# Moving the norm chains, the token sums and two groups of loads by hand in a one-core decoder layer

## The chip, the core and the metric

One NeuronCore of a Trainium2 chip runs one layer of a hybrid decoder as one program. The metric is the device time of a launch in microseconds. The engines that matter here are TensorE (PE, matrix products), VectorE (DVE), ScalarE (ACT), GpSimd (POOL) and the queue of SyncE (SP), which issues most loads and stores. Each engine works through its own list in order; semaphores tie the lists together.

## The reference, cut to what matters

All arithmetic is fp32. The attention part, which the change does not touch, yields a mixed row `m` per token. What follows is this:

```python
xp = xp + rms_norm(m @ w_o, norm_mix_post)            # 1024 x 1024
h = rms_norm(xp, norm_ffn_pre)
z = h @ w_in                                          # 1024 x (2 * 2816)
g, u = split(z, 2)
c = sum(conv_w[j] * g_padded[:, j:j + T] for j in range(3)) + conv_b
y = (gelu(c) * u) @ w_out                             # 2816 x 1024
y_out = xp + rms_norm(y, norm_ffn_post)
```

`rms_norm(x, g)` is `x * rsqrt(mean(x*x) + eps) * g`, with the mean over a token's 1024 features.

## The kernel before

The 1032 tokens (1024 of the prompt, 8 samples) lie along the free axis, in three segments `s` = 0, 1, 2 of 344; the features lie on the 128 partitions in eight blocks `d`. A factor of a product is split into two reduced-precision parts (`wh`, `wl` for weights, `hh`, `hl` for rows), and each product takes three matmuls. One block of 128 outputs by one segment is therefore 24 matmuls (8 blocks of the contraction, 3 each), which the text calls a unit.

**Output projection.** For each segment, eight units `ps_o` are computed (d = 0..7). ACT copies each result to `mix`, squares it, and POOL adds the square to `acc`.

**The norm chain** of a segment, the generator `norms_stage(s, acc, mix)`, then does: `rstd_1` (PE sums `acc` over the partitions into `n`; DVE scales it to `ms`; POOL takes the power -1/2, `rr`; DVE splits that into `rs` and builds the diagonal matrices `dg`), `rstd_2` (two matmuls spread the diagonals over all partitions, `bc`), then for each d `mix *= bc`, `x1 = x + mix` (even d on POOL, odd d on DVE) and the squares into `acc2`; then `rstd_1` and `rstd_2` again, and for each d `ht = x1 * g * bc`, its rounded part `hh[s]` (ACT) and the rest `hl[s]` (DVE). The text calls the four PE pieces of the chain of segment s n1(s), bc1(s), n2(s) and bc2(s). The `yield`s let the caller weave the chain into the products: two steps after each unit, and what is left at the end of a segment.

**The MLP's opening.** `ffn_in(j, s, ...)` computes a gate unit `gp` and an up unit `up` for column block j and segment s. It runs for j = 0, 1 on segments 0 and 1 with chain 2 woven in, then for j = 0, 1 on segment 2. Between them stand the **token sums**: from the rows of segments 0 and 1 (`hh`, `hl`), POOL forms for each of k = 0..3 the sums `tt` which `put` splits into `tw[0..2]` (ACT rounds, DVE subtracts) and back into `hh[1]`. The block loop j = 2..21 (`block`) needs `tw`, and weight sums `S1..S4` that POOL forms and `put` splits into `ww`.

**The last stage** multiplies by `w_out` (`ps_y`, loads by `load_t` and `load_n`: weights `wyraw`, rows `ar`). The chains of its two parts, `finish(part, acc, fv, x1)`, scale `fv` on DVE, add `x1y` on POOL and store `yT` on the SP queue, behind which the next loads stand.

Where nothing fixes it, a scheduler orders each engine's list. Before the change PE's list is in program order only from the block loop on.

Of the kernel before, what the change touches and what calls it, by code (L numbers as in the profile page):

```python
# [51 lines left out]
def step_kernel(ctx: ExitStack, tc: tile.TileContext, gam, g128, xT, w_in, w_o, w_f, w_y, norms, ngb, cst, subln,  # L52
# [777 lines left out]
    def norms_stage(s, acc, mix):  # L830

        yield
        dg = rstd_1(pw, acc)
# [30 lines left out]
        for d in range(ND):  # L864
            t = pw.tile([P, SEG], F32, tag="sq", bufs=3, name="ht")
            nc.vector.scalar_tensor_tensor(t, x1[:, d, :], gn[:, 2, d:d + 1], bc, ALU.mult, ALU.mult)
            nc.scalar.activation(a[:, d, 2:SEG + 2], t, AF.Copy)
            nc.vector.tensor_tensor(b[:, d, 2:SEG + 2], t, a[:, d, 2:SEG + 2].bitcast(F32), ALU.subtract)
            if d % 2 and d < ND - 1:
                yield  # L870
# [4 lines left out]
    chain = None
    rot = 0
    w_all = [*w2, split_w(load_w(w_o[2]), wo, "o", bufs=6)]
    for s in range(3):
# [3 lines left out]
        for d in range(ND):  # L882
# [13 lines left out]
            add_sq(pw, acc, ps, d == 0, nc.gpsimd)  # L896
            if chain is not None and (d, s) not in first:
                next(chain, None)
                next(chain, None)
        if chain is not None:  # L900
            for _ in chain:
                pass
        chain = norms_stage(s, acc, mix)
# [64 lines left out]
    for j in range(2):  # L968
        for s in range(2):
            for _ in ffn_in(j, s, *wj[j]):  # L970
                next(chain, None)
                next(chain, None)
    for _ in chain:
        pass
# [9 lines left out]
    def part(t, s, k):
        return t[s][:, k, 2:SEG + 2].bitcast(F32)

    def put(hi, lo, t):
        nc.scalar.activation(hi, t, AF.Copy)  # L988
        nc.vector.tensor_tensor(lo, t, hi.bitcast(F32), ALU.subtract)  # L989

    for k in range(4):
        b12, b22, t1, t2, t3 = (tt.tile([P, SEG], F32, tag=f"tt{i}", name=f"tt{i}") for i in range(5))
        G = nc.gpsimd.tensor_tensor
        G(b12, part(hh, 1, k), part(hl, 1, k), ALU.add)
        G(b22, part(hh, 1, 4 + k), part(hl, 1, 4 + k), ALU.add)
        G(t3, b22, b12, ALU.subtract)
        put(tw[1][:, 0, k], tw[1][:, 1, k], t3)
        G(t1, b12, part(hh, 0, k), ALU.subtract)
        G(t1, t1, part(hl, 0, k), ALU.subtract)
        G(t2, b22, t1, ALU.subtract)  # L1000
        put(tw[0][:, 0, k], tw[0][:, 1, k], t2)
        G(b12, part(hh, 0, 4 + k), t2, ALU.subtract)
        G(b12, b12, part(hl, 0, 4 + k), ALU.add)
        put(tw[2][:, 0, k], tw[2][:, 1, k], b12)
        put(hh[1][:, k, 2:SEG + 2], hl[1][:, k, 2:SEG + 2], t1)
# [397 lines left out]
```

## Time and profile before

| what | value |
|---|---|
| time, median of 3 runs | 1395.82 us (1395.66 to 1395.98) |
| the profiled execution's own time | 1393.19 us |
| its span | 1391.1 us |
| mean granted TensorE clock | 0.985 |
| busy: PE / DVE / ACT / POOL | 1317.4 / 980.6 / 574.4 / 494.7 us |

The profile records one execution. Its span runs from the first to the last instruction; the execution's own time has 2.1 us more around it. That execution was 2.6 us below the median of the runs, so a sum that is made on the span is carried to the median by differences. Times in the rows are microseconds from the start of the span.

### The profile page before, as it was taken

Reading aid. Unit: us, or ns where it says so; the run is one execution under the profiler, and the core shown is the slowest. Engines: PE = TensorE matmul, PEld = TensorE weight load, DVE = VectorE, ACT = ScalarE, POOL = GpSimd, SP = SyncE. Lnnn points to the kernel's source line nnn. Section 1 sums busy time; section 2 is a strip of 40 time slices with the busy share of each in tenths; the row PEclk is TensorE's granted clock in tenths of the full one; section 3 lists DMA queues with packets and bytes.
Section 4 is the critical chain, followed back from the end, with each engine's and each line's share of the span. In section 5 each row is a group of like instructions: output and inputs, shape, how many; then the busy total and the mean of one; then the engine's idle time right before and its main releaser. Section 6 shows DMA issues by size and latency. Waiting matters only on the chain.

```text
span 1391.1 us, 22792 instructions
## 1 busy us (share of the span) xinstructions
PE 1317.4 (95%) x8235; PEld 1270.0 (91%) x8235; DVE 980.6 (70%) x1832; ACT 574.4 (41%) x1148; POOL 494.7 (36%) x402
## 2 busy tenths in 40 slices
PE   6999989999999999998879999999999999989998
PEld 5999888888999999998879999999999999989976
DVE  7665759879688865478777777777777655565575
ACT  6254425335222145354344443443443345536544
POOL 5300356745545621444652332332432200140140
PEclk9999999999999999999989999999999999999999
DMA  5334275764564534233022222121122277667674
GB/s 220 118 102 134 85 238 195 218 202 126 163 192 142 176 120 160 71 113 109 29 92 79 81 97 74 69 91 68 70 91 69 84 259 261 211 210 251 188 235 156
DMA packets 96915, 196.51 MB, mean 141 GB/s; under 512 B 17306, under 2 KB 47130, under 8 KB 96418
## 3 DMA queue, kind: packets, MB, share of 16 engines
q1 hardware_dynamic: 90082, 183.45, 40.6%
q10 hardware_dynamic: 6720, 11.62, 2.3%
q8 instruction: 64, 1.05, 0.3%
q14 instruction: 49, 0.40, 0.1%
HBM read 155.11 MB, written 30.48 MB: 133 GB/s over the span
## 4 chain that ended last, share of the span: by engine, by line
PE 66%; DVE 16%; POOL 7%; DMA 5%; issue 4%; ACT 2%; SPq 0%; DVEq 0%; POOLq 0%; ACTq 0%
PE ps_y L1213 4%; PE ps_in L114 4%; PE ps_y L1212 4%; PE ps_y L1214 4%; PE ps_in L116 4%; PE ps_in L115 4%; DVE acc_v L587 3%; PE pb L1021 3%; PE pb L1020 3%; PE pb L1022 3%; PE up L1022 2%; PE pc L1021 2%; PE pc L1022 2%; PE up L1021 2%; PE pc L1020 2%
## 5 line engine op out<-in xcount | busy, mean ns | idle before, releaser
L114 PE MATMUL ps_in<-xh,wh 128*128 128x344 f32 x672 | 224.8, 335 | 6.8 <-ACT xh L193 5.9
L115 PE MATMUL ps_in<-xl,wh 128*128 128x344 f32 x672 | 221.2, 329 | 1.9 <-DVE xl L194 1.9
L116 PE MATMUL ps_in<-xh,wl 128*128 128x344 f32 x672 | 220.0, 327 | 1.1 <-DVE wl L109 1.1
L114 PEld LDWEIGHTS ps_in<-xh,wh 128*128 128x128 f32 x672 | 130.2, 194 | 9.9 <-ACT xh L193 5.9
L1153 DVE TENSOR_TENSOR wyl<-wyraw,wyh 128x1024 fp32r<-128x1024 f32 x66 | 83.7, 1271 | 74.1 <-ACT wyh L1152 71.8
L115 PEld LDWEIGHTS ps_in<-xl,wh 128*128 128x128 f32 x672 | 130.1, 194 | 4.4 <-DVE xl L194 3.6
L161 POOL TENSOR_TENSOR acc<-acc,sq 128x344 f32<-128x344 f32 (+1 forms) x56 | 59.0, 1054 | 208.8 <-ACT sq L160 203.9
L116 PEld LDWEIGHTS ps_in<-xh,wl 128*128 128x128 f32 x672 | 130.0, 193 | 1.6 <-DVE wl L109 1.4
L1212 PE MATMUL ps_y<-ah,wyh 128*128 128x388 f32 x352 | 120.2, 341 | 4.4 <-ACT ah L1163 4.4
L1039 POOL TENSOR_TENSOR S<-wraw 128x512 f32<-128x512 f32 x20 | 33.0, 1652 | 252.3 <-DMA wraw<-in_w_f 237.8
L1213 PE MATMUL ps_y<-al,wyh 128*128 128x388 f32 x352 | 120.1, 341 | 1.2 <-DVE al L1164 1.2
L1214 PE MATMUL ps_y<-ah,wyl 128*128 128x388 f32 x352 | 119.6, 340 | 0.0
L494 POOL TENSOR_TENSOR pg<-pg,qb 128x512 f32<-128x512 f32 x64 | 91.2, 1447 | 37.5 <-DMA pg<-in_kpool 26.9
L1152 ACT ACTIVATE wyh<-wyraw 128x1024 fp32r<-128x1024 f32 x66 | 69.7, 1058 | 73.8 <-PE ps_y L1213 43.5
L989 DVE TENSOR_TENSOR ww<-S,ww 128x512 fp32r<-128x512 f32 x80 | 88.6, 1125 | 9.1 <-ACT ww L988 9.1
L988 ACT ACTIVATE ww<-S 128x512 fp32r<-128x512 f32 x80 | 50.6, 634 | 94.2 <-POOL S L1040 33.9
L989 DVE TENSOR_TENSOR ww<-wraw,ww 128x512 fp32r<-128x512 f32 x80 | 75.2, 941 | 19.2 <-ACT ww L988 17.6
L1020 PE MATMUL pb<-tw,ww 128*128 128x344 f32 x240 | 77.3, 322 | 10.9 <-ACT tw L988 10.2
L988 ACT ACTIVATE ww<-wraw 128x512 fp32r<-128x512 f32 x80 | 50.1, 627 | 86.8 <-PE up L1022 63.4
L1164 DVE TENSOR_TENSOR al<-ar,ah 128x388 fp32r<-128x388 f32 (+2 forms) x110 | 60.5, 564 | 25.8 <-ACT ah L1163 24.9
L1021 PE MATMUL pb<-tw,ww 128*128 128x344 f32 x240 | 77.3, 322 | 0.8 <-DVE tw L989 0.8
L1022 PE MATMUL pb<-tw,ww 128*128 128x344 f32 x240 | 76.9, 321 | 0.0
(324 smaller groups left out, 3841.6 us busy)
## 6 DMA issues: line engine op xcount, KB each, us to landing
wyraw<-in_w_y SPq DMA_DIRECT2D x66, 512.0 KB, 3.8
wraw<-in_w_f SPq DMA_DIRECT2D x44, 512.0 KB, 3.2
pg<-in_kpool SPq DMA_DIRECT2D x64, 256.0 KB, 3.0
pg<-in_vpool SPq DMA_DIRECT2D x64, 256.0 KB, 2.7
wraw<-in_w_in SPq DMA_DIRECT2D x27, 512.0 KB, 4.1
ar<-ad SPq DMA_DIRECT2D x44, 194.0 KB, 3.8
ad<-cc SPq DMA_DIRECT2D x20, 344.0 KB, 2.3
ar<-ad SPq DMA_DIRECT2D x44, 150.0 KB, 3.3
```

The lines of the kernel that those rows point to most:

```text
L114: nc.tensor.matmul(ps, lhsT=wh[:, k, :], rhs=ah[:, k, n0:n1], start=(first and i == 0), stop=False)
L115: nc.tensor.matmul(ps, lhsT=wh[:, k, :], rhs=al[:, k, n0:n1], start=False, stop=False)
L116: nc.tensor.matmul(ps, lhsT=wl[:, k, :], rhs=ah[:, k, n0:n1], start=False, stop=(last and i == len(order) - 1))
L494: nc.gpsimd.tensor_tensor(kp, kp, qb.rearrange("p (a b) -> p a b", b=P), ALU.mult)
L988: nc.scalar.activation(hi, t, AF.Copy)
L989: nc.vector.tensor_tensor(lo, t, hi.bitcast(F32), ALU.subtract)
L1020: nc.tensor.matmul(ps, lhsT=w[:, 0, k], rhs=bh, start=(first and k == 0), stop=False, skip_group_check=True)
L1021: nc.tensor.matmul(ps, lhsT=w[:, 0, k], rhs=bl, start=False, stop=False, skip_group_check=True)
L1022: nc.tensor.matmul(ps, lhsT=w[:, 1, k], rhs=bh, start=False, stop=(last and k == 3), skip_group_check=True)
L1212: nc.tensor.matmul(pss[d], lhsT=wh[:, i, w], rhs=ah, start=(f == 0), stop=False)
L1213: nc.tensor.matmul(pss[d], lhsT=wh[:, i, w], rhs=al, start=False, stop=False)
L1214: nc.tensor.matmul(pss[d], lhsT=wl[:, i, w], rhs=ah, start=False, stop=(f == NF - 1))
```

## The change

It has five parts. (1) `rstd_1` builds all diagonals with one broadcast multiplication instead of two instructions per 128 columns. (2) `norms_stage` keeps `x` in four tiles of two rows with four buffers, each loaded and stored by itself, in place of one tile with one buffer; its squares have two buffers and `ht` two of its own; for segment 1 the rows before rounding stay as `h1`; for segment 2 the odd `hl` are subtracted on POOL. (3) The steps of a chain are set by a table, `STEPS`, one entry per unit behind the chain's start; chains may overlap; PE's list is in program order from the output projection on, with a list of accumulator banks written out. (4) The opening runs over segments outside and column blocks inside; the token sums are formed from `h1` with six POOL instructions per k instead of nine, k = 0, 1, 2 behind the units 3, 4 and 6 of the opening and k = 3 behind the chain; POOL's list there is in program order. (5) `finish` issues the store of row d - 2 behind the addition of row d.

```diff
-        dg = pl.tile([P, 2, n], F32R, tag="dg", bufs=1, name="dg")
-        for b, (c, w) in enumerate(blks):
-            for i in range(2):
-                nc.vector.tensor_scalar(dg[:, i, c:c + w], ident[:, 0:w], rs[:, i, b:b + 1].bitcast(F32), None,
-                                        ALU.mult)
-        return dg
+        dg = pl.tile([P, 2 * nb, P], F32R, tag="dg", bufs=1, name="dg")
+        nc.vector.tensor_tensor(dg, ident.unsqueeze(1).broadcast_to([P, 2 * nb, P]),
+                                rs.bitcast(F32).rearrange("p a b -> p (a b)").unsqueeze(2)
+                                .broadcast_to([P, 2 * nb, P]), ALU.mult)
+        return dg.rearrange("p (a b) c -> p a (b c)", a=2)[:, :, 0:n]
...
-        x1 = pw.tile([P, ND, SEG], F32, tag="x1", name="x1")
-        nc.sync.dma_start(x1, xT[s])
+        xp = [pw.tile([P, 2, SEG], F32, tag="x1", bufs=4, name="x1") for _ in range(4)]
+        x1 = [xp[d // 2][:, d % 2] for d in range(ND)]
+        for i in range(4):
+            nc.sync.dma_start(xp[i], xT[s, :, 2 * i:2 * i + 2])
...
+            (nc.gpsimd if s == 2 and d % 2 else nc.vector).tensor_tensor(
+                b[:, d, 2:SEG + 2], t, a[:, d, 2:SEG + 2].bitcast(F32), ALU.subtract)
...
+    STEPS = [{0: 1, 2: 2, 3: 2, 6: 1, 8: 2, 9: 2}] * 2 + [{0: 1, 2: 2, 3: 2, 5: 1, 7: 4}]
+    chains = []
+    def unit_done():
+        for ch in list(chains):
+            for _ in range(STEPS[ch[2]].get(ch[1], 0)):
+                next(ch[0], None)
+            ch[1] += 1
...
+    def token_sums(k):
+        t1, t2, t3, t4 = (tt.tile([P, SEG], F32, tag=f"tt{i}", bufs=(4 if i == 0 else 2), name=f"tt{i}")
+                          for i in range(4))
+        G = nc.gpsimd.tensor_tensor
+        G(t1, h1[k], hh[0][:, k, 2:SEG + 2].bitcast(F32), ALU.subtract)
+        G(t1, t1, hl[0][:, k, 2:SEG + 2].bitcast(F32), ALU.subtract)
+        t1s.append(t1)
+        G(t2, h1[4 + k], t1, ALU.subtract)
+        put(tw[0][:, 0, k], tw[0][:, 1, k], t2)
+        G(t3, h1[4 + k], h1[k], ALU.subtract)
+        put(tw[1][:, 0, k], tw[1][:, 1, k], t3)
+        G(t4, hh[0][:, 4 + k, 2:SEG + 2].bitcast(F32), t2, ALU.subtract)
+        G(t4, t4, hl[0][:, 4 + k, 2:SEG + 2].bitcast(F32), ALU.add)
+        put(tw[2][:, 0, k], tw[2][:, 1, k], t4)
+    for s in range(2):
+        for j in range(2):
+            for _ in ffn_in(j, s, *wj[j]):
+                unit_done()
+                if u in (3, 4, 6):
+                    token_sums({3: 0, 4: 1, 6: 2}[u])
+                u += 1
+    for ch in chains:
+        for _ in ch[0]:
+            pass
+    token_sums(3)
...
             nc.gpsimd.tensor_tensor(x1[:, d, :], x1[:, d, :], fv[:, d, :], ALU.add)
+            if d > 1:
+                nc.sync.dma_start(yT[part, :, d - 2, :], x1[:, d - 2, :])
+            yield
+        for d in (ND - 2, ND - 1):
             nc.sync.dma_start(yT[part, :, d, :], x1[:, d, :])
-            yield
```

Three places show how the lists move. The first is POOL's list in the opening, around the end of chain 2's additions. Before, the power `rr` of n2(2) came right behind the four even rows of `x1`, and the second group of token sums behind it:

```order
L842 TENSOR_TENSOR x1_8095<-x1_8095,mix_7825 128x344
L842 TENSOR_TENSOR x1_8095<-x1_8095,mix_7904 128x344
L131 TENSOR_TENSOR rr_8258<-ms_8256,ct_71 128x3
L994 TENSOR_TENSOR tt0_8394<-hh_7912,hl_7913 128x344
L996 TENSOR_TENSOR tt4_8398<-tt1_8395,tt0_8394 128x344
```

Of the change, the four even rows of `x1` are followed by the token sums of k = 0 and 1, twelve instructions. The piece below begins at the ninth of them; `rr` of n2(2) stands behind the twelfth, and the sums of k = 2 stand ahead of the odd `hl` of segment 2.

```order
L994 TENSOR_TENSOR tt1_8233<-h1_8068,tt0_8232 128x344
L996 TENSOR_TENSOR tt2_8234<-h1_8068,h1_8006 128x344
L998 TENSOR_TENSOR tt3_8235<-hh_7668,tt1_8233 128x344
L999 TENSOR_TENSOR tt3_8235<-tt3_8235,hl_7669 128x344
L131 TENSOR_TENSOR rr_8287<-ms_8285,ct_71 128x3
L991 TENSOR_TENSOR tt0_8319<-h1_8010,hh_7668 128x344
L992 TENSOR_TENSOR tt0_8319<-tt0_8319,hl_7669 128x344
L994 TENSOR_TENSOR tt1_8320<-h1_8072,tt0_8319 128x344
L996 TENSOR_TENSOR tt2_8321<-h1_8072,h1_8010 128x344
L998 TENSOR_TENSOR tt3_8322<-hh_7668,tt1_8320 128x344
L999 TENSOR_TENSOR tt3_8322<-tt3_8322,hl_7669 128x344
L871 TENSOR_TENSOR hl_8371<-ht_8378,hh_8370 128x344
```

What moved: `rr`, for which n2(2)'s chain waits, is now behind twelve token sums, and the rest of that chain behind six more.

The second is DVE's list there. Before, the last square of chain 2 was added (`acc`) ahead of the token sums' `tw`:

```order
L842 TENSOR_TENSOR x1_8095<-x1_8095,mix_7957 128x344
L161 TENSOR_TENSOR acc_8097<-acc_8097,sq_8185 128x344
L931 SCALAR_TENSOR_TENSOR c_8244<-gp_8194,cwt_7978,c_8244 128x344
L161 TENSOR_TENSOR acc_8097<-acc_8097,sq_8190 128x344
L932 SCALAR_TENSOR_TENSOR c_8244<-gp_8194,cwt_7978,c_8244 128x344
L989 TENSOR_TENSOR tw0_8367<-tt3_8376,tw0_8367 128x344
```

Of the change, two `tw` of k = 0 stand ahead of the last `acc`:

```order
L841 TENSOR_TENSOR x1_8111<-x1_8111,mix_7919 128x344
L983 TENSOR_TENSOR tw0_7962<-tt1_8192,tw0_7962 128x344
L983 TENSOR_TENSOR tw1_7963<-tt2_8193,tw1_7963 128x344
L160 TENSOR_TENSOR acc_8116<-acc_8116,sq_8187 128x344
L942 SCALAR_TENSOR_TENSOR c_8273<-gp_8207,cwt_7924,c_8273 128x344
```

Further on, the three `tw` of k = 2 and the returned rows of segment 1 stand between the diagonals of n2(2) and the first row `ht` of segment 2:

```order
L136 TENSOR_TENSOR dg_8292<-ct_71,rs_8289 128x768
L983 TENSOR_TENSOR tw0_7962<-tt1_8320,tw0_7962 128x344
L983 TENSOR_TENSOR tw1_7963<-tt2_8321,tw1_7963 128x344
L983 TENSOR_TENSOR tw2_7964<-tt3_8322,tw2_7964 128x344
L941 SCALAR_TENSOR_TENSOR c_8360<-gp_8294,cwt_7924,c_8360 128x344
L983 TENSOR_TENSOR hl_7999<-tt0_8191,hh_7998 128x344
L942 SCALAR_TENSOR_TENSOR c_8360<-gp_8294,cwt_7924,c_8360 128x344
L983 TENSOR_TENSOR hl_7999<-tt0_8232,hh_7998 128x344
L983 TENSOR_TENSOR hl_7999<-tt0_8319,hh_7998 128x344
L948 TENSOR_TENSOR c_8360<-c_8360,up_8335 128x344
L869 SCALAR_TENSOR_TENSOR ht_8374<-x1_8108,gn_69,bc_8367 128x344
```

What moved is the order of `tw` against `acc` and `ht`; ACT's list has the two matching roundings ahead of the last square too.

The third is the SP queue in the last stage, part 0, where the rows `ad8`, `ae8`, `ad9`, `ae9` feed two blocks of the contraction. Before:

```order
L1169 DMA wyraw_13788<-in_w_y 128x1024
L1145 DMA out_yT<-x1y_12649 128x388 x2
L1176 DMA ar_13790<-ad8_84 128x300
L1145 DMA out_yT<-x1y_12649 128x388 x2
L1177 DMA ar_13790<-ae8_106 128x80
L1176 DMA ar_13790<-ad9_85 128x300
L1177 DMA ar_13790<-ae9_107 128x80
L1145 DMA out_yT<-x1y_12649 128x388 x2
L1169 DMA wyraw_13841<-in_w_y 128x1024
```

Of the change:

```order
L1188 DMA wyraw_13752<-in_w_y 128x1024
L1162 DMA out_yT<-x1y_12622 128x388 x2
L1195 DMA ar_13754<-ad8_84 128x300
L1196 DMA ar_13754<-ae8_106 128x80
L1195 DMA ar_13754<-ad9_85 128x300
L1196 DMA ar_13754<-ae9_107 128x80
L1162 DMA out_yT<-x1y_12622 128x388 x2
L1188 DMA wyraw_13805<-in_w_y 128x1024
```

The stores of rows 2 and 3 have moved from ahead of `ae8` to behind `ae9`, and so two stores fewer stand ahead of the next `wyraw`.

## Rows read from the trace of the kernel before

**Rows 1.** PE's waits, 540 to 720 us: total, number, longest, us.

```profile
PE pb L1020 <- ACT tw L988: 10.2, 2, 8.3
PE bc L146 <- DVE dg L138: 9.1, 5, 4.6
```

**Rows 2.** Windows: busy us by engine, granted clock, DMA share, GB/s; sum of 560:720.

```profile
sum 160.00, PE 137.17 PEld 133.48 DVE 111.18 ACT 67.08 POOL 81.83; mean PE 17.15 PEld 16.68 DVE 13.90 ACT 8.38 POOL 10.23
...
648.00:650.00 2.00, 2.00 (x9) 2.00 (x9) 2.00 (x6) 1.51 (x4) 1.58 (x2) 0.50 0.26 88
702.00:708.00 6.00, 5.01 (x16) 4.64 (x17) 4.91 (x9) 2.37 (x5) 2.21 (x3) 0.50 0.31 96
```

**Rows 3.** Timeline of PE around a wait: start, duration, in brackets the idle time before.

```profile
641.26 0.32 PE L114 MATMUL gp<-hh,wh 128*128 128x346 f32 x1
641.42 0.32 PE L115 MATMUL gp<-hl,wh 128*128 128x346 f32 x1
646.30 0.60 PE L146 MATMUL bc<-dg,ones_r 128*128 128x344 f32 x2 [4.57 <-DVE dg L138]
...
647.68 0.49 PE L114 MATMUL up<-hh,wh 128*128 128x344 f32 x1
647.97 0.49 PE L115 MATMUL up<-hl,wh 128*128 128x344 f32 x1
```

**Rows 4.** Groups by line, 540 to 720 us: count, busy us, mean ns, idle before.

```profile
L868 DVE TENSOR_TENSOR hl<-ht,hh 128x344 fp32r<-128x344 f32 x24 | 12.6, 569 | 1.7 <-ACT hh L867 1.7
L842 POOL TENSOR_TENSOR x<-x,mix 128x344 f32<-128x344 f32 x12 | 12.5, 1047 | 15.9 <-DVE mix L841 15.8
L996 POOL TENSOR_TENSOR tt<-tt,tt 128x344 f32<-128x344 f32 x4 | 5.5, 1366 | 0.3
L999 POOL TENSOR_TENSOR tt<-tt,hl 128x344 f32<-128x344 f32 x4 | 3.7, 934 | 0.3
```

**Rows 5.** Timelines of DVE and POOL, 612 to 616 us.

```profile
612.26 1.34 DVE L841 TENSOR_TENSOR mix<-mix,bc 128x344 f32<-128x344 f32 x3
614.07 1.24 DVE L161 TENSOR_TENSOR acc<-acc,sq 128x344 f32<-128x344 f32 x1
613.73 1.20 POOL L161 TENSOR_TENSOR acc<-acc,sq 128x344 f32<-128x344 f32 x1
```

**Rows 6.** Timeline of DVE: the diagonals, and one instruction of 1024 columns.

```profile
645.20 1.22 DVE L138 TENSOR_SCALAR dg<-ct,rs 128x128 fp32r<-128x128 f32 x6
1342.29 1.23 DVE L1153 TENSOR_TENSOR wyl<-wyraw,wyh 128x1024 fp32r<-128x1024 f32 x1 [0.60 <-ACT wyh L1152]
```

**Rows 7.** The chain that ended last, near 604 us: start, us, what.

```profile
603.84 5.71 DMA x<-in_xT
```

**Rows 8.** Timelines of POOL, SP, ACT and PE in the last stage, part 0.

```profile
1224.84 3.50 POOL L1144 TENSOR_TENSOR x1y<-x1y,fv 128x388 f32<-128x388 f32 x1
1228.31 4.05 POOL L1144 TENSOR_TENSOR x1y<-x1y,fv 128x388 f32<-128x388 f32 x1
1228.81 0.38 SPq L1176 DMA_DIRECT2D ar<-ad  x1
1232.39 1.29 SPq L1145 DMA_DIRECT2D out_yT<-x1y  x2
1233.73 0.42 SPq L1177 DMA_DIRECT2D ar<-ae  x1
1236.16 0.40 SPq L1169 DMA_DIRECT2D wyraw<-in_w_y  x1
1236.14 0.52 ACT L1163 ACTIVATE ah<-ar 128x380 fp32r<-128x380 f32 x1 [7.12 <-DMA ar<-ae]
1240.98 1.06 ACT L1152 ACTIVATE wyh<-wyraw 128x1024 fp32r<-128x1024 f32 x1 [3.54 <-DMA wyraw<-in_w_y]
1236.71 0.44 PE L1212 MATMUL ps_y<-ah,wyh 128*128 128x388 f32 x1 [4.39 <-ACT ah L1163]
```

**Rows 9.** Timeline of PE in the last stage, part 1.

```profile
1338.95 0.50 PE L1253 MATMUL ps_n<-wyl,ah 128*128 128x512 f32 x1 [1.51 <-DVE wyl L1153]
```

More of the change, by code (lines that the diff above doesn't have):

```diff
@@ L841, in norms_stage @@
             nc.vector.tensor_tensor(mix[d], mix[d], bc, ALU.mult)
-            (nc.vector if d % 2 else nc.gpsimd).tensor_tensor(x1[:, d, :], x1[:, d, :], mix[d], ALU.add)
-            add_sq(pw, acc2, x1[:, d, :], d == 0, nc.vector)
+            (nc.vector if d % 2 else nc.gpsimd).tensor_tensor(x1[d], x1[d], mix[d], ALU.add)
+            add_sq(pw, acc2, x1[d], d == 0, nc.vector, bufs=2)
             if d % 2:
+                nc.scalar.dma_start(x1d[:, d - 1:d + 1, s * SEG:(s + 1) * SEG], xp[d // 2])
+            if d % 2 and d < ND - 1:
                 yield
-        nc.scalar.dma_start(x1d[:, :, s * SEG:(s + 1) * SEG], x1)
-        yield
-        yield
         yield
         dg = rstd_1(pw, acc2)
-        yield
         yield
@@ L863, in norms_stage @@
             nc.vector.tensor_copy(b[:, :, 0:2], hl[-1][:, :, SEG:SEG + 2].bitcast(F32))
[L864 to L870, printed above, removed]
         hh.append(a)
         hl.append(b)
-        yield
-    chain = None
+        for d in range(ND):
+            if s == 1:
+                t = pw.tile([P, SEG], F32, tag="h1", bufs=8, name="h1")
+                h1.append(t)
+            else:
+                t = pw.tile([P, SEG], F32, tag="ht", bufs=2, name="ht")
+            nc.vector.scalar_tensor_tensor(t, x1[d], gn[:, 2, d:d + 1], bc, ALU.mult, ALU.mult)
+            nc.scalar.activation(a[:, d, 2:SEG + 2], t, AF.Copy)
+            (nc.gpsimd if s == 2 and d % 2 else nc.vector).tensor_tensor(
+                b[:, d, 2:SEG + 2], t, a[:, d, 2:SEG + 2].bitcast(F32), ALU.subtract)
+            if d % 2:
+                yield
+    h1 = []
+    STEPS = [{0: 1, 2: 2, 3: 2, 6: 1, 8: 2, 9: 2}] * 2 + [{0: 1, 2: 2, 3: 2, 5: 1, 7: 4}]
[5 more added lines that the diff above has]
+            ch[1] += 1
+    fixed = tc.manual_schedule(engines={mybir.EngineType.PE})
+    fixed.__enter__()
+    tags = iter(("S", "o", "mm", "mm", "S", "o", "mm", "o", "mm", "S", "S", "S",
+                 "mm", "o", "mm", "S", "S", "S", "mm", "o"))
     rot = 0
@@ L889, in step_kernel @@
                     w_all.append(split_w(load_w(w_o[d + 1]), wo, "o", bufs=6))
-                ps = bank(("mm", "S", "S", "mm", "S")[rot % 5], "ps_o")[:, 0:SEG]
-                rot += 1
+                ps = bank(next(tags), "ps_o")[:, 0:SEG]
                 prod3(ps, *w, mh, ml, order, 0, SEG)
@@ L895, in step_kernel @@
             mix.append(mx)
[L896 to L903, printed above, removed]
+            add_sq(pw, acc, ps, d == 0, nc.gpsimd, bufs=2)
+            if (d, s) not in first:
+                unit_done()
+        chains.append([norms_stage(s, acc, mix), 0, s])
     cwt = ft.tile([P, NF, 3], F32, name="cwt")
@@ L967, in step_kernel @@
     wj = [wpair(0), wpair(1)]
[L968 to L974, printed above, removed]
-    closed(pw_cm)
-    LO, HI = slice(0, 4), slice(4, 8)
-    tb = [slice(2, SEG + 2)] * 2
     tw = [f1.tile([P, 2, 4, SEG], F32R, name=f"tw{i}") for i in range(3)]
     t_cm, tt = opened("tt")
-    def part(t, s, k):
-        return t[s][:, k, 2:SEG + 2].bitcast(F32)
     def put(hi, lo, t):
@@ L989, in put @@
         nc.vector.tensor_tensor(lo, t, hi.bitcast(F32), ALU.subtract)
-    for k in range(4):
[L992 to L1005, printed above, removed]
+    t1s = []
+    def token_sums(k):
[12 more added lines that the diff above has]
+        put(tw[2][:, 0, k], tw[2][:, 1, k], t4)
+    pool = tc.manual_schedule(engines={mybir.EngineType.Pool})
+    pool.__enter__()
+    u = 0
+    for s in range(2):
+        for j in range(2):
+            for _ in ffn_in(j, s, *wj[j]):
+                unit_done()
+                if u in (3, 4, 6):
[5 more added lines that the diff above has]
+    token_sums(3)
+    closed(pool)
+    for k in range(4):
+        put(hh[1][:, k, 2:SEG + 2], hl[1][:, k, 2:SEG + 2], t1s[k])
     closed(t_cm)
+    closed(pw_cm)
+    LO, HI = slice(0, 4), slice(4, 8)
     def side_b(s, k0):
@@ L1118, in step_kernel @@
     src = sums(load_j(3))
-    fixed = tc.manual_schedule(engines={mybir.EngineType.PE})
-    fixed.__enter__()
     for j in range(2, NF):
@@ L1144, in finish @@
             nc.gpsimd.tensor_tensor(x1[:, d, :], x1[:, d, :], fv[:, d, :], ALU.add)
+            if d > 1:
+                nc.sync.dma_start(yT[part, :, d - 2, :], x1[:, d - 2, :])
+            yield
+        for d in (ND - 2, ND - 1):
             nc.sync.dma_start(yT[part, :, d, :], x1[:, d, :])
-            yield
     def split_y(raw, pl=None, bufs=2):
```

1 line of the change is left out of this document (removed).

## The prediction

> **What bounds the kernel now.** I read PE's waits first, since PE is busy nearly all of the span and a change pays only where PE stands still. In the stretch of the output projection and the opening it is busy 137.2 of 160 us, so 22.8 are idle [rows 2]. Two waits make most of them [rows 1]: block 2 waits for token sums (`pb <- tw`, 10.2, longest 8.3) and the chains' broadcasts wait for diagonals (`bc <- dg`, 9.1, longest 4.6). Second, what a wait costs afterwards. Behind the 4.57 us gap matmuls follow each other 0.29 us apart in place of 0.16 [rows 3], at a granted clock of 0.50 [rows 2], half of 2.4 GHz. Some 11 matmuls were slow there and about 22 behind the 8.3 us gap (the stretch at 0.50 up to 708 us, rows 2), 0.13 us each: 1.4 + 2.9 = 4.3 us. So 27.1 us can be had in this stretch. A unit is 24 matmuls of 0.16, 3.8 us.
>
> Third, the last stage, where PE stands 4.39 us on `ah`, which waits for `ar <- ae` [rows 8]. The SP queue shows why: that load was issued at 1233.73 behind two stores that waited for POOL's addition ending at 1228.31 + 4.05 = 1232.36. In part 1 there is a gap of 1.51 us [rows 9].
>
> **The change, part by part.** I walk the new lists, from durations of this trace. A POOL row takes 0.93 (`tt` L999) to 1.37 us (L996); I take 1.05, as `x` L842 [rows 4]. A DVE row takes from 0.45 us (three `mix` in a row 1.34, rows 5) to 0.57 (`hl`, rows 4).
>
> *Chains 0 and 1.* The old single `x` tile held up chain 1: its load stands 5.71 us in the chain that ended last [rows 7]. Four tiles remove that wait. Then DVE is the limit: between bc1(1) and n2(1) lie 16 `ht`/`hl` of chain 0 and 19 `mix`, `x`, `acc` of chain 1, 35 rows at 0.54 = 18.8 us, against four units of PE, 15.2: PE waits 3.6 (1.6 at 0.48 a row). bc1(1) now stands directly behind bc2(0); `dg` has one buffer, so its diagonals follow bc2(0)'s 0.60 us [rows 3], and three weight splits stand ahead of them, the last of which waits for a load. Diagonals and hand-over make 1.1 without that load; with the split behind it (1.23, rows 6) I take 2.2, and 3.1 if the load is late. n1(1) adds 0.2. Sum 6.0.
>
> *Chain 2 and the token sums.* Count from T, when bc2(1) runs. PE reaches bc1(2) at T + 8.7 and n2(2) at T + 20.6 (three units later). DVE's rows let POOL finish the fourth even `x1` at T + 20.4. Then POOL runs token sums, ACT rounds the first two and DVE subtracts them before the last square: POOL's fourth sum ends at 20.4 + 4 x 1.05 = T + 24.6, and rounding, square and addition make T + 26.2. n2(2) waits 5.6. `rr` stands behind the twelfth sum (T + 33.0) and waits for `ms`, which stands behind `tw2` of k = 1 at T + 34.6; with `rr`, `rs` and `dg` bc2(2) starts at T + 37.3 instead of T + 28.8. Loss so far 8.5, in which the half clock behind n2(2) is hidden, since POOL sets the time.
>
> Now PE has nothing else: the next unit needs `hh[2]`. POOL does six more sums (35.5 to T + 41.8), DVE `tw2`, then three `hl` and three `c` (2.7): first `ht` at T + 45.2, first row for PE at T + 46.2, 8.4 after bc2(2). The rows then come in pairs 2.0 us apart, because an odd row passes `ht` (0.5), ACT (0.45), POOL (1.05) and frees one of two `ht` buffers: the last at T + 53.7. That unit ends at T + 54.1 and not at T + 41.6: loss 12.5, and 1.4 of half clock behind it. Block 2 then finds `tw` and `ww` ready, three units later; the old waits on `tw`, `c` and `u` go.
>
> Sum of the stretch: 6.0 + 8.5 + 12.5 + 1.4 = 28.4 lost, against 27.1 before: **1.3 us slower**. Between the ends of the prices: 22 POOL rows (18 sums, 4 `hl`) at 0.93 give 2.5 back, DVE 2.0, the load 1.1, the clock 1.4, so 7.0 better; at 1.37 the POOL rows cost 7.0 more.
>
> The Trainium skill's page "SBUF — State Buffer" (SBUF: two separate sides) says that a DVE instruction with two SBUF inputs and a GpSimd instruction lock the same port pair against each other for a whole instruction. The trace agrees as far as DVE's `acc` of 1.24 us starts 0.34 into POOL's 1.20 and ends 0.38 behind it [rows 5]; by the page alone, an estimate, each DVE row between would push POOL's chain by its whole length, which is the slower rival below.
>
> *The diagonals in one instruction.* Six took 1.22 us; one DVE row of 1024 columns takes 1.23, so 768 columns take some 0.9 [rows 6], 0.3 less. Below: 0 if two broadcast inputs cost more, above 0.5. It is on PE's path at the first stage's three broadcasts and the two of `finish`: 5 x 0.3, of which I count **0.8 us saved**, since in the first stage a weight split of 1.2 now stands ahead of one. The page "VectorE: DVE Perf Modes" (The perf-mode tier table) speaks against this edit: scaling by a column's scalar runs two fp32 elements a cycle, a product of tensors one. By its rate, an estimate, 768 columns cost 0.8 us and the fixed part, which still beats six instructions.
>
> *The stores of `finish`.* Part 0 [rows 8]: `ad8` was issued at 1228.81, `ae8` 4.9 later; now `ae8`, `ad9` and `ae9` follow `ad8` at once, a good 0.4 apart, so `ae8` goes at 1229.3 and lands as before 2.4 later (1233.73 to 1236.14): 1231.7. PE runs dry at 1232.3 and so does not stop for `ah`. But the next `wyraw` still stands behind the stores of rows 2 and 3, whose additions end at 1232.36 and some 1.5 later. I take 1234.3, where it was 1236.16; that load took 4.8 us (to `wyh` at 1240.98), so `wyh` starts at 1237.7 (3.4 us) to 1239.1 (4.8) and PE, which has 4.25 us of matmuls, stops again at 1236.9 until 1238.8 to 1240.2, with 0.9 more for `wyl`. The block after began at 1243.3; now at about 1240.0: **3.3 us saved**, between 0.5 (all of it handed on, with a slow clock) and 5. Part 1's gap ends on DVE's `wyl`, and DVE is busy there with as many rows as before: **0.5**, 0 to 2.
>
> Total: +1.3 - 0.8 - 3.3 - 0.5 = -3.3 us, so 1389.9 where the profiled execution took 1393.19. The median of the runs is 2.6 higher: **1392.5**.
>
> **The rivals.** 0.2% is 2.8 us, about what a measurement of this kernel can tell from no change. (a) *As summed*, 1392.5 (1390 to 1394.5): 0.42. (b) *The new waits are shorter.* POOL rows at 0.93, the load early, DVE at 0.48 a row, no half clock: 7.0 better, 1385.5, and 1382 with `finish` and part 1 at their best. The sums now overlap chain 2, where POOL stood idle 15.9 us ahead of `x` [rows 4]; against it, every one stands ahead of something PE waits for. 0.17. (c) *Only moved.* `finish` hands its stall on whole and saves 0.5, part 1 nothing: +1.3 - 0.8 - 0.5 = 0, so 1395.8. For it speaks that POOL's addition took 3.50 and 4.05 us there, so that stores wait however they are placed [rows 8]. 0.19. (d) *Slower:* POOL is held up by DVE in the opening, as in those two additions. With 22 rows at 1.37, 1392.5 + 7.0 = 1399.5. From a mean of 1.05 + 3.3/22 = 1.20 us on the gain is gone, and from 1.33 it is slower by 0.2%. For it: eight DVE rows in the wait region; against it, DVE there mostly waits for POOL. 0.22.
>
> **How the numbers follow.** Faster by over 0.2% needs under 1393.0: most of (a), 0.30, all of (b), 0.17, and a little of the others, 0.05: 0.52. Within 0.2%: 0.12 of (a), 0.14 of (c), 0.02 of (d): 0.28. Slower: the rest, 0.20. Eight in ten lie from 1382, the end of (b), to 1401, above (d).
>
> **What would show it.** Right: PE waits of 3 to 5 us at n2(1), 4 to 7 at n2(2) on DVE's `acc`, and one of 7 to 10 for the first `hh` of segment 2, with `gp` behind it paced by POOL's `hl`; none on `tw`; in the last stage no wait for `ar <- ae` but one of 2 to 3 for `wyh` one pair later. Wrong: no wait at n2(2), or POOL's sums above 1.3 us each, or the broadcast diagonals above 1.2 us.

## The result, and the profile after

The changed kernel takes **1405.2 us** (median of 6 runs, 1402.5 to 1408.6), the kernel before 1395.7 in the same session: ratio 1.0073, 95% interval 1.005 to 1.0096. That is 9.5 us slower; 1392.5 was forecast, with 1401 as the upper end. The profiled execution took 1404.38 us with a span of 1402.6, which is 11.5 more than the span before.

Three stretches divide that span: up to the first `ps_o` matmul (518.4 before, 519.4 after), from there to the last `pa` matmul of the block loop (588.7 before, 602.0 after), and from there to the last output store, the tail (280.9 and 278.1). So the middle stretch lost 13.3 us and the tail won 2.8. The 1.0 of the first stretch tells nothing: over the sixteen profiles of this text the first `ps_o` starts anywhere from 515.2 to 524.6. The columns of these rows are minimum, median and maximum duration in ns, then the first and the last start:

```profile
L114 PE MATMUL ps_o<-mh,wh x192: 313/320/634, 519.4 to 639.2; 128*128 128x344 f32 x192
L1038 PE MATMUL pa<-hh,ww x160: 314/319/326, 709.1 to 1121.4; 128*128 128x344 f32 x160
```

PE's waits from 540 to 720 us, which answer to [rows 1]:

```profile
PE n L127 <- DVE acc L160: 8.0, 1, 8.0
PE gp L114 <- ACT hh L870: 7.6, 1, 7.6
PE n L127 <- DVE n L125: 6.3, 1, 6.3
PE gp L1038 <- DVE c L948: 4.0, 1, 4.0
PE bc L145 <- DVE dg L136: 1.1, 1, 1.1
PE n L127 <- POOL acc L160: 0.7, 1, 0.7
PE gp L115 <- POOL hl L871: 0.7, 2, 0.4
```

The waits of before on `tw` are gone, and that on diagonals is 1.1 us long. In their place stand n2(1) with 8.0, n2(2) with 6.3, the first `hh` of segment 2 with 7.6, and one that was not forecast, 4.0 on `c` inside block 2. The windows answer to [rows 2] (busy us by engine with counts, granted clock, DMA share, GB/s):

```profile
597.00:599.00 2.00, 1.86 (x11) 1.86 (x12) 0.24 (x2) 0.00 (x0) 1.72 (x3) 0.72 0.03 8
599.00:601.00 2.00, 2.00 (x9) 2.00 (x9) 1.94 (x5) 0.00 (x0) 0.03 (x1) 0.50 0.00 0
...
634.00:636.00 2.00, 2.00 (x9) 2.00 (x9) 1.36 (x3) 0.46 (x1) 1.92 (x3) 0.50 0.00 0
636.00:638.00 2.00, 2.00 (x8) 2.00 (x8) 1.31 (x2) 0.00 (x0) 1.92 (x2) 0.50 0.00 0
...
716.00:718.00 2.00, 2.00 (x9) 2.00 (x8) 0.28 (x1) 0.00 (x0) 0.00 (x0) 0.50 0.80 238
...
sum 160.00, PE 131.30 PEld 127.71 DVE 97.87 ACT 63.53 POOL 70.21; mean PE 16.41 PEld 15.96 DVE 12.23 ACT 7.94 POOL 8.78
```

PE is idle 28.7 us of the 160 (22.8 before). But it is also slow more often: 0.50 is 1.2 of 2.4 GHz. PE's timeline, where the bracket is the idle time before:

```profile
595.76 0.66 PE L127 MATMUL n<-ct,acc 128*128 128x1 f32 x6
597.14 0.76 PE L127 MATMUL n<-ct,acc 128*128 128x1 f32 x6 [0.73 <-POOL acc L160]
606.93 0.48 PE L145 MATMUL bc<-dg,ones_r 128*128 128x344 f32 x2
608.46 0.58 PE L145 MATMUL bc<-dg,ones_r 128*128 128x344 f32 x2 [1.05 <-DVE dg L136]
632.10 1.31 PE L127 MATMUL n<-ct,acc 128*128 128x1 f32 x6 [7.97 <-DVE acc L160]
634.27 0.49 PE L114 MATMUL ps_o<-mh,wh 128*128 128x344 f32 x1
634.56 0.49 PE L115 MATMUL ps_o<-ml,wh 128*128 128x344 f32 x1
643.44 0.47 PE L145 MATMUL bc<-dg,ones_r 128*128 128x344 f32 x2
670.12 1.30 PE L127 MATMUL n<-ct,acc 128*128 128x1 f32 x6 [6.27 <-DVE n L125]
681.26 0.48 PE L145 MATMUL bc<-dg,ones_r 128*128 128x344 f32 x2
689.37 0.66 PE L114 MATMUL gp<-hh,wh 128*128 128x346 f32 x1 [7.62 <-ACT hh L870]
715.12 0.63 PE L1038 MATMUL gp<-hh,ww 128*128 128x346 f32 x1 [3.98 <-DVE c L948]
```

Counted in this timeline, matmuls that start 0.29 us after the one before instead of 0.16 follow n1(1) (12 of them), n2(1) (18), n2(2) (16), the first `hh` (9) and the `gp` of block 2 (18): 73, against 11 + 15 = 26 before. At 0.13 each that is 9.5 us and 3.4. Idle time 5.9 more and half clock 6.1 more are 12.0 of the 13.3 us; Most of the rest lies in the products `n` themselves: 36 matmuls, busy 6.1 us in place of 4.9.

Why n2(1) waits is seen on the SP queue, POOL and DVE:

```profile
609.47 8.04 SPq L837 DMA_DIRECT2D x<-in_xT  x3
626.10 0.33 SPq L837 DMA_DIRECT2D x<-in_xT  x1
```

```profile
629.12 1.23 POOL L841 TENSOR_TENSOR x<-x,mix 128x344 f32<-128x344 f32 x1 [4.43 <-DMA x<-in_xT]
```

```profile
607.45 0.96 DVE L136 TENSOR_TENSOR dg<-ct,rs 128x768 fp32r<-128x768 f32 x1 [0.32 <-PE bc L145]
624.99 1.04 DVE L869 SCALAR_TENSOR_TENSOR ht<-x,gn,bc 128x344 f32<-128x344 f32 x2
713.37 0.55 DVE L942 SCALAR_TENSOR_TENSOR c<-gp,cwt,c 128x336 f32<-128x336 f32 x1
714.47 0.51 DVE L948 TENSOR_TENSOR c<-c,up 128x336 f32<-128x336 f32 x1 [0.34 <-ACT c L947]
```

The fourth load of chain 1's `x` goes at 626.10, after the last two `ht` of chain 0 (624.99 to 626.0), whose rows it overwrites; POOL stands 4.43 us for it. The four tiles together hold no more rows than the one tile did. And chain 0's rows are late: bc2(0) stands behind whole units now and runs 11.2 us after n2(0), where it came 3.9 after it before (592.61 to 596.54).

The last stage, PE, which answers to [rows 8, 9]:

```profile
1249.12 0.44 PE L1232 MATMUL ps_y<-al,wyh 128*128 128x388 f32 x1 [1.94 <-DVE al L1183]
1251.07 0.69 PE L1233 MATMUL ps_y<-ah,wyl 128*128 128x388 f32 x1 [1.51 <-DVE wyl L1172]
1350.06 0.50 PE L1272 MATMUL ps_n<-wyl,ah 128*128 128x512 f32 x1 [1.63 <-DVE wyl L1172]
```

The wait of 4.39 on `ah` is gone, and one of 3.45 in two pieces stands one pair of blocks later.

### The profile page after: what moved, and what is told of

It reads as the page before. It is cut to its first block, busy times and chain, and to the rows that moved or that the text cites. A ratio compares the mean times of both kernels' runs of the same rounds, so it can differ in the third digit from the quotient of the medians.

```text
span 1402.6 us, 22787 instructions
## 1 busy us (share of the span) xinstructions
PE 1322.3 (94%) x8235; PEld 1274.8 (91%) x8235; DVE 970.8 (69%) x1769; ACT 575.4 (41%) x1148; POOL 484.4 (35%) x398
## 4 chain that ended last, share of the span: by engine, by line
PE 65%; DVE 16%; POOL 7%; DMA 5%; issue 4%; ACT 2%; SPq 0%; POOLq 0%; DVEq 0%; ACTq 0%
PE ps_y L1233 4%; PE ps_y L1231 4%; PE ps_y L1232 4%; PE ps_in L114 4%; PE ps_in L115 3%; PE ps_in L116 3%; DVE acc_v L586 3%; PE pb L1039 3%; PE pb L1040 3%; PE pb L1038 3%; PE gp L1038 2%; PE gp L1040 2%; PE gp L1039 2%; PE up L1040 2%; PE pc L1039 2%
## 5 line engine op out<-in xcount | busy, mean ns | idle before, releaser
L114 PEld LDWEIGHTS ps_in<-xh,wh 128*128 128x128 f32 x672 | 129.3, 192 | 12.8 <-ACT xh L192 6.0
L493 POOL TENSOR_TENSOR pg<-pg,qb 128x512 f32<-128x512 f32 x64 | 90.8, 1442 | 40.6 <-DMA pg<-in_kpool 30.7
L108 ACT ACTIVATE wh<-wraw 128x1024 fp32r<-128x1024 f32 (+1 forms) x41 | 42.5, 1036 | 88.2 <-PE ps_in L115 36.9
L1183 DVE TENSOR_TENSOR al<-ar,ah 128x388 fp32r<-128x388 f32 (+2 forms) x110 | 63.7, 590 | 20.3 <-ACT ah L1182 19.7
L1038 PE MATMUL pb<-tw,ww 128*128 128x344 f32 x240 | 77.2, 322 | 0.0
L1039 PE MATMUL pb<-tw,ww 128*128 128x344 f32 x240 | 77.2, 322 | 0.0
```

Of the source, the lines that this page charges most:

```text
L114: nc.tensor.matmul(ps, lhsT=wh[:, k, :], rhs=ah[:, k, n0:n1], start=(first and i == 0), stop=False)
L493: nc.gpsimd.tensor_tensor(kp, kp, qb.rearrange("p (a b) -> p a b", b=P), ALU.mult)
L1038: nc.tensor.matmul(ps, lhsT=w[:, 0, k], rhs=bh, start=(first and k == 0), stop=False, skip_group_check=True)
L1039: nc.tensor.matmul(ps, lhsT=w[:, 0, k], rhs=bl, start=False, stop=False, skip_group_check=True)
```

## The experiments

Theory A: the opening loses because chain 1's `x` waits for chain 0's late rows, because the token sums stand ahead of chain 2's rows, and because each wait is followed by matmuls at half clock. Rivals: `x` waits for the SP queue; POOL's rows are slower than counted; POOL's odd `hl` pace segment 2; a small part of the change (stores, diagonals) costs the time. Ratios are to the kernel before on the same chip, with 95% intervals; "stretch" and "tail" are the second and the third of the three above, from one profile each. The stretch is 588.3 to 588.8 in the three versions that keep the old opening. The tail scatters more: 275.0 to 278.5 in the thirteen versions that share the changed tail.

**The two small parts alone, on the kernel before.** The stores of `finish` moved (the last hunk of the change), and the diagonals in one instruction (its first hunk).

> The kernel before with only the stores of the last stage moved (row d - 2 stored behind the addition of row d). The prediction counted 3.3 + 0.5 us for them. Theory (the stall is handed on): the 4.39 us wait for ah in part 0 goes, a new one of 1.5 to 3 us for wyh, al or wyl stands one pair later; in all 1 to 3 us faster than before, ratio 0.998 to 0.9993. Rival (the stores cost nothing net): within 1 us of before. Rival (the changed kernel's loss sits here): 3 us or more slower, ratio over 1.002.

> The kernel before with only the diagonals built by one broadcast product. Theory: one instruction takes 0.95 us where six took 1.22, so the five diagonals on TensorE's path save 0.8 us in all; ratio 0.998 to 1.001. Rival (the list of VectorE's work is reordered by it and a weight or row split comes first): the first stage loses 1 us or more, its first multiplication of the output projection starts later than 519.0 us, ratio over 1.0007.

Stores alone: 1393.4 us, 0.9988 (0.9964 to 1.0012), tail 276.6; no wait on `ah`, but 0.65 and 1.03 on the weights, and 1.86 in part 1. Diagonals alone: 1391.2 us, 0.9979 (0.9962 to 0.9996), stretch 588.8 and tail 277.2. Neither costs the time. Their tails are 4.3 and 3.7 shorter than the one of before, and the changed kernel's, with both edits, 2.8. With a scatter of 3.5 among equal tails these single profiles don't say how much each edit brings.

**x from another queue.**

```diff
-            nc.sync.dma_start(xp[i], xT[s, :, 2 * i:2 * i + 2])
+            nc.gpsimd.dma_start(xp[i], xT[s, :, 2 * i:2 * i + 2])
```

> The changed kernel with the loads of x issued from GpSimd's queue instead of SP's, so that the fourth load of a segment no longer stands behind a weight load that waits for its buffer. Theory (that load makes n2(1) late): the wait at n2(1) falls from 7.97 us to 2 to 4.5, the half clock behind it goes, 5 to 8 us faster than the changed kernel, so about 1.001 to 1.004 of before. Rival (the four tiles hold no more rows than the one did, so the load waits for chain 0's last rows in any queue): n2(1) still waits 6 us or more and the time stays within 2 us of the changed kernel, 1.006 to 1.009. Rival (VectorE's list is the limit, as the prediction had it): 3.5 us stay there, with VectorE busy all through.

1405.6 us, 1.0064 (1.0041 to 1.0086); n2(1) waits 8.90 and comes 114.2 us behind the first `ps_o`, where it came 112.7 behind it in the changed kernel. The rival falls. POOL's timeline says for what the fourth load waits, now that no queue is ahead of it:

```profile
629.18 0.55 POOL L837 DMA_DIRECT2D x<-in_xT  x1 [2.06 <-DVE ht L869]
```

**x in one tile again** (the other hunks of part 2 kept).

```diff
-        xp = [pw.tile([P, 2, SEG], F32, tag="x1", bufs=4, name="x1") for _ in range(4)]
+        xp = pw.tile([P, ND, SEG], F32, tag="x1", name="x1")
```

> The changed kernel with one edit of part 2 undone: x lies in one tile again, one load and one store per segment. The prediction said that four tiles remove chain 1's wait for x; the run showed n2(1) waiting 7.97 us behind the fourth load, so either the tiles bring nothing (theory A: the load of a segment waits for the late rows of chain 0 either way; n2(1) again at 632 +- 1 us and a time of 1405 +- 2), or they do overlap most of the load and the 7.97 is what is left (theory B): one load can then start only when the last ht of chain 0 has run, at 625.0, takes about 5.7 us, and eight additions, squares and sums follow, some 7 us, so that n2(1) runs at 637 to 641, 5 to 9 us later, and the time is 1410 to 1415.

1405.7 us, 1.0064 (1.0038 to 1.0091), stretch 603.9; n2(1) at 632.85 in place of 632.10 (1.4 us later when both are counted from the first `ps_o`), with 4.82 and 4.12 of PE's idle time ahead of it. So the time is as theory A had it, but not the way: DVE's list now has all of chain 0's rows first, so that the load goes at 615.1 and is waited for at once:

```profile
618.31 0.18 DVE L859 CAST hl<-hl 128x16 fp32r<-128x16 f32 x1
620.94 3.96 DVE L840 TENSOR_TENSOR x<-x,mix 128x344 f32<-128x344 f32 x4 [2.44 <-DMA x<-in_xT]
```

Together with that new order, the number of tiles is worth nothing that this can tell.

**bc2(0) one unit earlier.**

```diff
-    STEPS = [{0: 1, 2: 2, 3: 2, 6: 1, 8: 2, 9: 2}] * 2 + [{0: 1, 2: 2, 3: 2, 5: 1, 7: 4}]
+    STEPS = [{0: 1, 2: 2, 3: 2, 6: 1, 7: 2, 8: 2}, {0: 1, 2: 2, 3: 2, 6: 1, 8: 2, 9: 2}] + [{0: 1, 2: 2, 3: 2, 5: 1, 7: 4}]
```

> The changed kernel with one number of the step table changed: chain 0's second broadcast bc2(0) and its rows come one unit earlier (after unit 7 and 8 of the chain, not 8 and 9), so no longer back to back with bc1(1). Theory (chain 0's rows come late, they hold the four tiles of x, so the last load of x of chain 1 cannot start, which makes n2(1) wait): chain 0's eight ht end some 4 us earlier, the last load of x too, and n2(1)'s wait falls from 8 us to 2 to 5; with the half clock behind it 5 to 9 us are won in the stretch from the first ps_o to the last pa, which takes 602.0 us in the changed kernel and 588.7 in the one before. Rival (VectorE has too many rows between, wherever the broadcast stands): the wait stays above 6.5 us and the stretch above 600.

1398.2 us, 1.0014 (0.9998 to 1.003); stretch 596.8, 5.2 less. Counted from the first `ps_o`, n2(1) comes 5.4 us earlier. It still waits 5.55, now with no stop of POOL for `x` and with DVE busy from 602 to 626 but for 1.2 us. So the late place of bc2(0) is shown as a cause, worth some 5 us, and behind it DVE is the limit. The edit also brings bc1(1) 2.9 us forward, which no longer stands right behind bc2(0); how much of the 5 us comes by that and how much by chain 0's rows and `x`, this run doesn't separate.

**n2(1) and n2(2) one unit later.**

```diff
-    STEPS = [{0: 1, 2: 2, 3: 2, 6: 1, 8: 2, 9: 2}] * 2 + [{0: 1, 2: 2, 3: 2, 5: 1, 7: 4}]
+    STEPS = [{0: 1, 2: 2, 3: 2, 6: 1, 8: 2, 9: 2}, {0: 1, 2: 2, 3: 2, 7: 1, 8: 2, 9: 2},
+             {0: 1, 2: 2, 3: 2, 6: 1, 7: 4}]
```

> The changed kernel with two numbers of the step table changed: n2(1) and n2(2) one unit later (unit 7 and 6 of their chains, not 6 and 5), everything else as it is. Theory (the table asks for the sum of squares before it can be there, and each such stop of 6 to 8 us also costs some 3 us of half clock behind it): n2(1) waits 4 us instead of 8 and n2(2) 2.5 instead of 6.3, without a half clock behind n2(2); the stretch from the first ps_o to the last pa falls from 602.0 to 590 to 597. Rival (the chain behind n2 comes later by the same unit and nothing is won): 600 to 604.

1397.7 us, 1.0007 (0.999 to 1.0023); stretch 595.3. n2(1) waits 3.77 and n2(2) 2.52, but bc2(2) then waits 7.24, and a wait of 3.77 is followed by half clock as the one of 7.97 is (0.50 from 631 to 637 us). The gain is the unit that PE does instead of waiting.

**The token sums behind chain 2, and split.** First all four k behind the chain; then the two instructions that need only the rows k of segments 0 and 1 early, the other four behind the chain, and all `hl` of segment 2 on DVE; then that with bc2(0) earlier.

```diff
-                if u in (3, 4, 6):
-                    token_sums({3: 0, 4: 1, 6: 2}[u])
...
-    token_sums(3)
+    for k in range(4):
+        token_sums(k)
```

> The changed kernel with all token sums behind chain 2 (none inside the opening's loop). Theory (GpSimd's 18 sums ahead of chain 2's end cost 8.5 us at n2(2) and bc2(2) and most of the wait for the first rows of segment 2, but are only moved by this): the waits at n2(2) and for hh of segment 2 fall from 6.3 and 7.6 us to under 1 and under 4, and a wait of 12 to 22 us for tw appears at block 2; in all within 4 us of the changed kernel, 1.004 to 1.010 of before. Rival (sums ahead of the chain are the whole loss, and behind it they are covered by the units of segment 2): 8 us or more faster than the changed kernel, under 1.002.

> The changed kernel with the token sums split: the part that needs only rows k of segments 0 and 1 (two of six instructions) for k = 0 to 2 behind the opening's first unit, the rest behind chain 2, and all hl of segment 2 on VectorE. Theory (sums ahead of chain 2's end cost TensorE 21 us, and behind it there is room for 16 to 18 of them before block 2 needs tw): n2(2) waits under 3 us, the first rows of segment 2 under 3, and block 2 under 5, so the stretch from the first ps_o to the last pa takes 588 to 595 us against 602.0. Rival (only moved, as in the run with all sums behind the chain): a wait of 8 us or more in block 2 and a stretch over 598.

> The two edits of the runs before this one together on the changed kernel. If their gains are of separate waits they add up: 5 to 9 and 7 to 14 us less than the changed kernel's 602.0 in the stretch, so 580 to 590, and the time is 0.992 to 1.000 of before. If one only uncovers the other, the stretch stays above 590.

All behind: 1405.6 us, 1.0074 (1.0052 to 1.0096). The waits at n2(2) and `hh` shrink to 2.14 and 1.37, and the loss stands at the block loop:

```profile
713.26 0.62 PE L1037 MATMUL pa<-hh,ww 128*128 128x344 f32 x1 [13.71 <-DVE cpt L945]
```

Split: 1400.6, 1.0028 (1.0012 to 1.0045). The block loop no longer waits, but the first `hh` waits 12.32: where the lists of DVE and ACT are free, the scheduler put the `tw` of the sums ahead of `ht`. With bc2(0) earlier 1394.3, 1.0001 (0.998 to 1.0022).

**Four of the six sums.** The subtraction and the addition of `hl[0]` are left out, so the sums lack those rests.

> The changed kernel with two of the six GpSimd instructions of each token sum left out (the two that carry the rounding rests, so tw and the returned rows are off by those rests). Theory (GpSimd's list sets the pace from n2(2) to the first rows of segment 2): six instructions fewer ahead of those rows at 1.05 us each make bc2(2) 4 us and the first gp of segment 2 6 us earlier after bc2(1) (46 us before, so 40). Rival (VectorE's or ScalarE's list sets it): under 3 us.

One run, 1399.3 us. The first `hh` came at T + 42.5 instead of T + 45.9, but bc2(2) at T + 40.6 instead of T + 37.8, and DVE's order had changed too. The first is less than expected and the second the other way: inconclusive on POOL's share there. The stretch was 593.4, 8.6 shorter, with waits of 1.36 at the first `hh` and 2.21 in block 2, so fewer sums do shorten the opening; by which engine's list this one run doesn't tell.

**All hl of segment 2 on DVE.**

```diff
-            (nc.gpsimd if s == 2 and d % 2 else nc.vector).tensor_tensor(
+            nc.vector.tensor_tensor(
```

> The changed kernel with all hl of segment 2 on DVE, POOL's four rows of them gone. By the prediction the rows of segment 2 come in pairs 2.0 us apart because odd rows pass POOL, which made 4.1 us of the loss between the first hh and the end of that unit. If so, the first hh stays where it is (wait of 7.6) and the first pa, 19.7 us behind it, comes 2 to 4 us earlier: 1401.5 to 1403.5. Rival: POOL's part costs nothing, since ACT's hh and DVE's ht pace the unit and the half clock behind the wait stretches its matmuls anyway: pa again 19 to 20 us behind the first hh, 1404 to 1406. A third way: DVE now carries four rows more and the first hh itself moves by 1 to 2 us.

1401.8 us, 1.0032 (1.0014 to 1.0051). From the first `hh` to the first `pa` it takes 20.4 us (694.78 to 715.2), 19.7 with POOL, so giving POOL's rows to DVE wins nothing. What they cost on POOL is not shown by it, since DVE's list now has two returned rows of segment 1 between those of segment 2. The fourth k's sums now ran on POOL ahead of the rows, `hh` waits 12.61, and the wait inside block 2 is gone; the ratio is lower than the changed kernel's 1.0073, with intervals that just touch, by a way that none of the three expected.

**Rows ahead of sums by program order, then everything together.** DVE's and ACT's lists are put in program order from bc2(2) on, with the sums split and `hl` one row behind `ht`; then both edits of `STEPS` as well (the diff is that of the second).

```diff
-    STEPS = [{0: 1, 2: 2, 3: 2, 6: 1, 8: 2, 9: 2}] * 2 + [{0: 1, 2: 2, 3: 2, 5: 1, 7: 4}]
+    STEPS = [{0: 1, 2: 2, 3: 2, 6: 1, 7: 2, 8: 2}, {0: 1, 2: 2, 3: 2, 7: 1, 8: 2, 9: 2},
+             {0: 1, 2: 2, 3: 2, 6: 1}]
...
+    late = tc.manual_schedule(engines={mybir.EngineType.DVE, mybir.EngineType.Activation})
+    late.__enter__()
     for ch in chains:
         for _ in ch[0]:
             pass
+    sums_a(3)
+    for k in range(4):
+        sums_b(k)
```

> The run with the split sums, with one more edit: VectorE and ScalarE in program order from bc2(2) on, so that the rows of segment 2 come ahead of the tw in their lists (in the run before the scheduler had put all tw ahead of the first ht, and TensorE waited 12.3 us for hh). Theory: that wait falls to under 2 us, and up to 8 us of it are won, since tw is needed only three units and two products later: stretch 586 to 592 against 597.8. Rival (block 2 then waits for tw or for a bank behind them as long): 596 or more.

> The run before with the step table of both earlier ones: bc2(0) one unit earlier, n2(1) and n2(2) one unit later. If the three causes are separate, n2(1) and n2(2) wait under 2 us each, hh under 2, no half clock behind n2: stretch 570 to 580, against 588.7 of the kernel before and 602.0 of the changed one; with the last stage as in the changed kernel the time is 0.985 to 0.993 of before. If one uncovers the other: 583 or more, 0.994 to 1.000.

The first: 1396.5, 1.0001 (0.9985 to 1.0017); the first `hh` waits 1.36 in place of 12.32. All together: **1382.8 us, 0.9895 (0.987 to 0.9919)**, stretch 582.3: it beats both kernels. Its waits from 540 to 720 us:

```profile
PE pa L1055 <- DVE usm L955: 5.5, 1, 5.5
PE n L127 <- DVE acc L160: 2.1, 2, 1.8
PE gp L114 <- ACT hh L875: 1.2, 1, 1.2
PE bc L145 <- DVE dg L136: 0.9, 1, 0.9
```

**One sum in six on DVE**, on top of that version.

```diff
-        G(t3, h1[4 + k], h1[k], ALU.subtract)
+        nc.vector.tensor_tensor(t3, h1[4 + k], h1[k], ALU.subtract)
```

> The fastest version so far (1382.8: the chain tables, the split sums and the rows ahead of the sums together) with the third of the six token sums of each k on DVE in place of POOL. What is left there is a wait of 5.5 us at the first pa on usm, behind POOL's last sums. If POOL's sums set it, four sums of 1.1 to 1.3 us fewer on POOL end it: the wait falls below 2 us and the time is 1378 to 1380. Rival: DVE, on which the four sums now stand with the rows that usm needs, is as late: the wait stays within 1 us of 5.5 and the time within 1382 to 1385.

1382.6 us, 0.988 (0.9853 to 0.9907), stretch 582.4: nothing won. The wait on `usm` is gone and one of 7.16 on `c` stands a little later. The rival holds on the time: DVE sets it.

## Why the prediction was wrong

**n2(1), the step that failed first.** "Four tiles remove that wait. Then DVE is the limit" gave 3.6 us. The wait was 7.97. DVE's rows were about as counted, but DVE also stood idle for 4.0 us between bc1(1) and n2(1), 1.1 of it on `x` and the rest on squares, the last 2.0 of those behind the fourth load (below); and it did a weight split of 1.53. What I missed is that tiles divide the rows without adding any: a load still waits for the rows of chain 0 that it replaces, and the change makes those late. The loads from another queue and in one tile left n2(1) within 1.5 us of where it was; bc2(0) one unit earlier brought 5 us.

```profile
630.91 1.14 DVE L160 TENSOR_TENSOR acc<-acc,sq 128x344 f32<-128x344 f32 x2 [1.32 <-ACT sq L159]
```

**The half clock, priced once.** I counted 1.4 us, behind the first `hh`, and called the half clock behind n2(2) hidden, although [rows 2, 3] showed what a wait costs. Measured are 9.5 us behind five waits, but not all of it was paid. Of the 2.1 behind n2(2) all but 0.5 were hidden, nearly as forecast, since the diagonals that bc2(2) needs ended at 680.74 and it ran at 681.26:

```profile
679.30 1.44 DVE L136 TENSOR_TENSOR dg<-ct,rs 128x768 fp32r<-128x768 f32 x1
```

The 1.6 behind n1(1) only took the place of waiting. In three versions with the same PE list up to there (the sums behind the chain, the rows ahead of the sums, `hl` on DVE) the same wait drew no half clock. There bc1(1) waited 2.1 to 2.2 instead of 1.05, and n2(1) came 112.2 to 112.7 us behind the first `ps_o`, as here (112.7). With `hl` on DVE:

```profile
598.90 0.76 PE L127 MATMUL n<-ct,acc 128*128 128x1 f32 x6 [0.84 <-POOL acc L160]
609.75 0.59 PE L145 MATMUL bc<-dg,ones_r 128*128 128x344 f32 x2 [2.12 <-DVE dg L136]
```

Paid and not priced were the 2.3 behind n2(1) and the 2.3 in block 2. Up to bc2(1) the measured sum is 9.75 us of waits (0.73, 1.05, 7.97) and 30 x 0.13 = 3.9 of half clock, 13.7 in place of 6.0. For the kernel before I had counted some 22 slow matmuls behind the wait of 8.3; its trace has 15, so the 27.1 us were 0.9 too many.

**Chain 2 and the sums: right.** Counted from T (643.44), n2(2) came at T + 26.7 (forecast 26.2) after 6.27 us (5.6), bc2(2) at T + 37.8 (37.3), the first `hh` at T + 45.9 (46.2) after 7.62 (8.4), the end of its unit at T + 54.2 (54.1), the first `pa` at T + 65.7 (54.1 + 1.4 + 11.4 = 66.9). The pacing by POOL's `hl` is there too. DVE stops for it before every odd row but the first, 2.1 us apart, and the last one ends at T + 53.7, as forecast:

```profile
692.97 0.57 DVE L869 SCALAR_TENSOR_TENSOR ht<-x,gn,bc 128x344 f32<-128x344 f32 x1 [0.53 <-POOL hl L871]
696.27 0.92 POOL L871 TENSOR_TENSOR hl<-ht,hh 128x344 fp32r<-128x344 f32 x1 [1.21 <-ACT hh L870]
```

Only the 1.4 us of half clock added behind that unit were not paid: its nine slow matmuls fell inside the time that the rows took anyway.

**Block 2: failed.** "Block 2 then finds `tw` and `ww` ready" looked past DVE, which still has `ww` and `tw` to subtract ahead of the `c` that frees PE's bank: 3.98 us, and 18 x 0.13 = 2.3 behind it.

So against the forecast: +7.7 up to T, -1.2 to the first `pa`, +6.3 behind it, 12.8 in all. The stretch was forecast at 1.3 slower and came 13.3 slower: 12.0 between them.

**Diagonals: right in size.** 0.96 us against 1.22 [rows 6], 0.3 less, though 1.44 at n2(2) beside a busy POOL, above the 1.2 that I had named as proof to the contrary.

**Finish: right in kind, the size open.** The stall was handed on one pair later as forecast, 3.45 us against 2 to 3, and part 1's gap stayed (1.63 against 1.51), so the 0.5 counted there did not come. The tail won 2.8 where 3.3 + 0.5 and 0.6 of diagonals were summed. Against the one tail of before, the thirteen changed ones win 2.4 to 5.9.

**The slower rival named another mechanism.** It wanted POOL rows at 1.37 us. The 24 rows of the sums took 24.8 us, 1.03 each, as the main sum had it, here the slowest and the fastest of their six groups (busy us, mean ns):

```profile
L994 POOL TENSOR_TENSOR tt<-h,tt 128x344 f32<-128x344 f32 x4 | 4.8, 1191 | 0.3
L991 POOL TENSOR_TENSOR tt<-h,hh 128x344 f32<-128x344 f32 x4 | 3.7, 927 | 0.0
```

None of my four cases made n2(1) longer or let each wait draw the half clock, so a time of 1405 had no case of its own.
